# A two-layer decoder trunk on one core: convolution accumulators in alternating banks, a later first mean, a fixed order for the layer norm, one modulation part moved to TensorE, other distances between tiles

## The chip, the cores and the metric

The kernel is one program on one core of a Trainium2 chip. Its time is the device time of one execution in microseconds (us). Engine names are those of the profile: PE is TensorE, DVE is VectorE, ACT is ScalarE, POOL is GpSimd, SP is SyncE, which here only issues DMAs.

## The reference

The input x has 256 rows (T) of 2048 channels (D); c is one conditioning vector. Two layers follow each other, the first with a convolution module, the second with attention; each is followed by a gated feed-forward (ffn) of inner width 5632.

```python
shift, scale, gate = split(silu(c) @ mod_w + mod_b, 3)       # once for each of four sub-layers
h = rms_norm(x) * g * (1 + scale) + shift
# layer 0, convolution module
u = h @ pw1_w + pw1_b;  u = val * sigmoid(gt)                 # halves of u, 2048 channels each
u = causal_depthwise_conv(u, width 31) + b
u = silu(layer_norm(u) * ln_g + ln_b)
y = u @ pw2_w + pw2_b;  x = x + gate * y
# ffn of both layers
u = causal_depthwise_conv(h @ up_w, width 3) + b
x = x + gate * ((silu(gt) * val) @ down_w)
```

Layer 1's mixer is stick-breaking attention with 16 heads (products qk, v and o). A last rms_norm gives the output.

## The kernel before

**Layout.** Channels lie on the 128 partitions, the 256 rows along the free dimension. So an activation is KD = 16 tiles of 128x256 (the inner ffn 44), and a weight matrix is a stream of blocks of 128x128. Eight blocks make a piece of 512 KB; pieces are loaded in a fixed order (`load_next`, six buffers `raw`).

**Products.** All products but pw1 run in three passes of a reduced format: `split_next` makes wh on ACT (L225) and wl = raw - wh on DVE (L226), four buffers each; activations are split likewise (hh and hl for the modulated input, zh and zl for pw2's, gh and gl for the down product's, oh and ol for o's). `gemm` issues wh·xh (L269), wh·xl (L270), wl·xh (L271) for each block. After every piece `tick` drives side work: it adds a rate (0.7 for pw2) to a credit, and each full credit calls `advance` on the list `fill`, which takes one step of the first `pace["fills"]` generators in it.

**Modulations.** The product silu(c) @ mod_w is made in two ways. Column-wise (`mod_part`), each 128 outputs are one 1024 KB load (in_mt) and one DVE multiply-and-reduce (L294). Row-wise (`mod_rows`), each chunk is one 1024 KB load (in_mr) and four matmul pairs on PE (L505); sixteen chunks make 2048 outputs, after which one step copies the sums (ACT, L510) and one turns them into columns (PE L514, DVE L518). `ROWS` says how many groups of 512 outputs of ffn0's shift are made row-wise: 2 of 4 before; the other eight column tiles go through `mod_part("ffn0", 0, 8)`. The generator `mods0` makes layer 0's gate (16 chunks, two closing steps), ffn0's scale (the same) and ffn0's shift. Loads of both kinds share three buffers, `mraw`. All loads are issued by SP in program order (`load`), so a load that waits for its buffer holds those behind it.

**The convolution** (L634 to L716). The first eight of pw1's sixteen output tiles are computed ahead, with four more pieces in front of the loop. Then a loop over c = 0..16 runs, each pass in 19 steps s. Of a tile's 31 taps, ACT makes the first (`conv_first`, L591, into PSUM), 19 follow on DVE (`conv_tap`, L595, accumulating in PSUM), and eleven products are made by ACT (`conv_prod`, L603) and summed by POOL (L679, L681). DVE's taps of tile c alternate with the second half of tile c-1's. PE has in a pass two pieces of pw1 (L572, at s = 0 and 9), a generator step at s = 2, in even passes one more at s = 11, and sums for the layer norm's mean (`y_sum`, L616) and squares (L632). `conv_sum` (L607, at s = 3) finishes tile c-2. `first_mean` (ACT L619, DVE L620) takes the mean of the first eight tiles at the start of pass 10; after it `y_centre` (L624) subtracts it from three tiles a pass. The gate of tile i >= 8 (`gate_act` on ACT, `gate_mul` on DVE) comes in pass min(2(i-8)+2, i-1) at s = 12 and 15, and needs pw1's pieces of that tile.

The accumulators of the taps are halves of two PSUM banks (`conv_banks`): before, tiles 0 and 1 share one bank, 2 and 3 the other, 4 and 5 the first again. Dependencies between engines are kept by bank: who writes one half waits for what was issued before on the other.

**Order.** The framework schedules instructions by priority and simulated readiness, except where `in_order(here)` chains all instructions of an engine issued since `here`: the convolution loop runs exactly as written. Each engine executes its own queue in order.

**After the loop**, eight generator steps, the layer norm's rstd (L378), and sixteen z tiles: t = y * rstd on POOL (L734), t - dm on DVE (L735), silu on ACT (L736), split in zh (ACT L344) and zl (DVE L345). Then pw2 runs, its first eight output tiles interleaved over z; `pw2_done` (L745, L746) updates x and starts the next ffn's input (L359, L411, L412).

**Distances of tiles.** `SKEW` pads the tiles of a kind by multiples of eight columns, (high part, low part): this sets how far apart in a partition the tiles lie that PE streams one after the other. `h_tile` pads every tile to T + 8 columns and the last high one by 24 more.

Of the kernel before, what the change touches and what calls it, by code (L numbers as in the profile page):

```python
# [16 lines left out]
P = 128  # L17
# [8 lines left out]

SKEW = {"h": (3, 0), "z": (1, 7), "g0": (4, 4), "g1": (2, 6), "o": (0, 3)}
HEAD = 16
UBUFS = 9
M0 = 8  # L30
MOD_AHEAD = 2
ROWS = 2

# [76 lines left out]
def hybrid_trunk(ctx: ExitStack, tc: tile.TileContext, cfg: Cfg, io: dict):  # L110
# [16 lines left out]
    def psum_acc():  # L127
        return acc.tile([P, 512], F32, name="ps")
# [39 lines left out]
    fill = []  # L168
    pace = {"rate": 0.0, "credit": 0.0, "side": 0.0, "steps": 0.0, "heads": 2, "fills": 1}

# [135 lines left out]

    def mod_part(m, part, first=0, all_of_it=True):
        ahead = []
# [7 lines left out]
        if part == 1:  # L316
            mod_scale(m, 0, KD)
        if all_of_it:
            have.add((m, part))
        yield  # L320
# [136 lines left out]
    with ExitStack() as cv:  # L457
# [62 lines left out]
        def mods0():  # L520
# [7 lines left out]
            yield  # L528
            yield from mod_rows(*rows_of[2])

        gb = cpool.tile([P, KD], F32, name="gb")
# [4 lines left out]
        hf = [h_tile("hh", kt)[:, :T].bitcast(F32) for kt in range(KD)]  # L536
        act_tables("sigmoid_and_others")
# [49 lines left out]
        def conv_first(j):  # L587
            if len(conv_banks) < 2 and j % 2 == 0:
                conv_banks.append(psum_b())
            conv_ps[j] = conv_banks[j // 2 % 2][:, j % 2 * T:(j % 2 + 1) * T]  # L590
            nc.scalar.activation(conv_ps[j], us[j % UBUFS][:, PADW:], AF.Identity, bias=pc("cdb", j, 1),  # L591
                                 scale=tap(j, PADW))
# [4 lines left out]

        prods = {}

        def conv_prod(j, i):  # L600
            pr = h_tile("hl", sum(prods.values()) % PRODUCTS)[:, :T].bitcast(F32)
            prods[j] = prods.get(j, 0) + 1
            nc.scalar.activation(pr, us[j % UBUFS][:, i:i + T], AF.Copy, scale=tap(j, i))  # L603
            return pr
# [7 lines left out]

        def y_sum(j):
            if j in (0, M0):
                st["b"] = psum_acc()
            nc.tensor.matmul(st["b"][:, :T], ones_d, ys[j], start=j in (0, M0), stop=j in (M0 - 1, KD - 1))  # L616

        def first_mean():
            nc.scalar.activation(m1, st["b"][:, :T], AF.Copy, scale=KD / M0)  # L619
            nc.vector.tensor_tensor(dm, st["b"][:, :T], m1, op=ALU.subtract)  # L620
            st["sq"] = psum_acc()
# [37 lines left out]
        conv_first(0)  # L659
        for _ in range(4):  # L660
            pw1_piece(next(pw1))
        for c in range(KD + 1):
            late = gates_at.get(c, [])
            if c == M0 + 2:
                first_mean()
# [6 lines left out]
            for s in range(nd):  # L672
# [21 lines left out]
                if s in (6, 10, 14) and c > M0 + 1 and centred < c - 1:  # L694
                    y_centre(centred)
                    squares.append(centred)
                    centred += 1
# [24 lines left out]
        nc.vector.tensor_tensor(dm, dm, st["b"][:, :T], op=ALU.add)  # L722
        var = t256()
# [7 lines left out]
        zs = []  # L731
        for j in range(KD):
            t = t256()
            nc.gpsimd.tensor_tensor(t, ys[j], rs, op=ALU.mult)  # L734
            nc.vector.tensor_tensor(t, t, dm, op=ALU.subtract)  # L735
            nc.scalar.activation(t, t, AF.Silu, bias=pc("ln_b", j, 1), scale=pc("ln_g", j, 1))  # L736
# [14 lines left out]
        drain(fill)  # L751
        have.add(("ffn0", 0))
        pace["fills"] = 1

# [312 lines left out]
```

## Time and profile before

| | us |
|---|---|
| median of three runs | 2392.74 (2390.23 to 2392.78) |
| the profiled execution's own time | 2390.86 |
| its span in the profile | 2389.1 |
| PE busy in it | 2310.8 (97%) |
| DVE busy in it | 1759.0 (74%) |
| granted clock of PE, mean | 0.99 |
| DMA, mean over the span | 253 GB/s |

In a row of the timeline, the first number is the start in us from the span's start, the second the length of the stretch; then engine, line, operation, written tile <- read tiles, shapes, and xN, the number of merged instructions; in square brackets the engine's idle time before and what ended it. A 32-bit matmul (L572, L505, L616, L632) is two instructions. In a row of windows, the stretch is followed by its length, the busy time and count of PE, PE's weight loads, DVE, ACT and POOL, the granted clock, the DMA engines' busy share and GB/s. Matmul ends are modelled, so counts of matmuls in a window say more than PE's busy time.

### The profile page before, as it was taken

The numbers are of one execution on the slowest core, as the hardware profiler recorded it, in microseconds if no ns is written. First come the engines' busy times: TensorE is split into PE (matmuls) and PEld (weight loads), VectorE is DVE, ScalarE is ACT, GpSimd is POOL, SyncE is SP. The second block draws the span as 40 slices with busy tenths as digits, with TensorE's granted clock in tenths as the row PEclk, the third lists the DMA queues.
The fourth block names the chain that finished last, engine by engine and source line by source line (L and its number), as shares of the span: only waits on it lengthen the run. The fifth ranks groups of instructions, "written<-read, shape, count | busy, mean of one in ns | idle before, by whom it ended". The sixth has DMA issues, their size and how long they took to land.

```text
span 2389.1 us, 44051 instructions
## 1 busy us (share of the span) xinstructions
PE 2310.8 (97%) x17812; PEld 2199.8 (92%) x17812; DVE 1759.0 (74%) x2386; ACT 1157.1 (48%) x1761; POOL 281.4 (12%) x361
## 2 busy tenths in 40 slices
PE   7999878999999999999999999999999999999997
PEld 5877646999999999999998999999999999999997
DVE  7687886798878778788887676788876555666554
ACT  2054553665553345555465545556555434555543
POOL 4056641200000000000121000121000000000011
PEclk9999989999999999999999999999999999999999
DMA  9987578577769878778866666676865556555553
GB/s 393 425 323 294 191 274 336 184 272 274 275 242 349 310 270 287 265 277 310 316 232 246 241 248 243 240 270 232 292 211 186 187 188 187 186 186 186 186 186 106
DMA packets 138302, 603.55 MB, mean 253 GB/s; under 512 B 15345, under 2 KB 15473, under 8 KB 113521
## 3 DMA queue, kind: packets, MB, share of 16 engines
q1 hardware_dynamic: 138098, 600.74, 70.4%
q8 instruction: 139, 2.28, 0.4%
q14 instruction: 65, 0.53, 0.1%
HBM read 598.58 MB, written 2.10 MB: 251 GB/s over the span
## 4 chain that ended last, share of the span: by engine, by line
PE 85%; DVE 8%; DMA 3%; issue 2%; ACT 1%; POOL 0%; DVEq 0%; SPq 0%; ACTq 0%; POOLq 0%
PE ps L271 25%; PE ps L269 24%; PE ps L270 24%; PE ps L572 5%; DMA mraw<-in_mt_mix 2%; DVE auxb L595 2%; DVE mraw L294 2%; DVE wl L226 1%; PE ps L901 1%; PE ps L902 1%; PE ps L903 1%; PE auxa L505 1%; DMA mraw<-in_mt_ffn 1%; PE auxb L572 0%; DVE hl L345 0%
## 5 line engine op out<-in xcount | busy, mean ns | idle before, releaser
L225 ACT CAST wh<-raw 128x1024 fp32r<-128x1024 f32 x688 | 720.8, 1049 | 869.9 <-PE ps L270 665.5
L226 DVE TENSOR_TENSOR wl<-raw,wh 128x1024 fp32r<-128x1024 f32 x688 | 842.3, 1227 | 396.1 <-ACT wh L225 385.8
L271 PE MATMUL ps<-hh,wl 128*128 128x256 f32 (+1 forms) x3328 | 937.8, 282 | 4.4 <-DVE wl L226 4.4
L270 PE MATMUL ps<-hl,wh 128*128 128x256 f32 (+1 forms) x3328 | 937.0, 282 | 3.0 <-DVE hl L345 1.5
L269 PE MATMUL ps<-hh,wh 128*128 128x256 f32 (+1 forms) x3328 | 936.0, 281 | 0.0
L271 PEld LDWEIGHTS ps<-hh,wl 128*128 128x128 f32 x3328 | 627.5, 189 | 5.0 <-DVE wl L226 5.0
L270 PEld LDWEIGHTS ps<-hl,wh 128*128 128x128 f32 x3328 | 627.8, 189 | 3.9 <-DVE hl L345 2.0
L269 PEld LDWEIGHTS ps<-hh,wh 128*128 128x128 f32 x3328 | 628.8, 189 | 0.4
L294 DVE CUSTOM_DVE_ANT_0 mraw<-mraw,csr 128x2048 f32<-128x2048 f32 x152 | 348.5, 2293 | 89.2 <-DMA mraw<-in_mt_mix 54.1
L271 PE MATMUL ps<-gh,wl 128*128 128x256 f32 x1408 | 399.7, 284 | 0.0
L269 PE MATMUL ps<-gh,wh 128*128 128x256 f32 x1408 | 397.7, 282 | 0.0
L270 PE MATMUL ps<-gl,wh 128*128 128x256 f32 x1408 | 393.5, 280 | 0.0
L270 PEld LDWEIGHTS ps<-gl,wh 128*128 128x128 f32 x1408 | 266.9, 190 | 0.0
L269 PEld LDWEIGHTS ps<-gh,wh 128*128 128x128 f32 x1408 | 266.0, 189 | 0.0
L271 PEld LDWEIGHTS ps<-gh,wl 128*128 128x128 f32 x1408 | 264.6, 188 | 0.0
L363 POOL TENSOR_TENSOR sumsq<-sumsq,t 128x256 f32<-128x256 f32 x56 | 59.8, 1068 | 1593.5 <-ACT t L359 1593.3
L572 PE MATMUL ps<-hh,raw 128*128 128x256 f32 x832 | 191.3, 383 | 0.0
L572 PEld LDWEIGHTS ps<-hh,raw 128*128 128x128 f32 x832 | 159.3, 192 | 27.8 <-issue 3.4
L770 DVE SCALAR_TENSOR_TENSOR t<-ps,par,t 128x254 f32<-128x254 f32 x336 | 160.2, 478 | 4.1
L595 DVE SCALAR_TENSOR_TENSOR auxb<-u,cpar,auxb 128x256 f32<-128x256 f32 x304 | 138.4, 485 | 8.9 <-ACT auxb L591 3.8
L681 POOL TENSOR_TENSOR y<-y,hl 128x256 f32<-128x256 f32 x144 | 108.4, 753 | 22.0 <-ACT hl L603 11.2
L767 ACT ACTIVATE t<-ps,par 128x256 f32<-128x256 f32 x168 | 93.7, 559 | 0.0
(168 smaller groups left out, 2120.9 us busy)
## 6 DMA issues: line engine op xcount, KB each, us to landing
raw<-in_w_down SPq DMA_DIRECT2D x176, 512.0 KB, 3.9
mraw<-in_mt_mix SPq DMA_DIRECT2D x80, 1024.0 KB, 8.0
mraw<-in_mt_ffn SPq DMA_DIRECT2D x72, 1024.0 KB, 6.0
raw<-in_w_pw SPq DMA_DIRECT2D x96, 512.0 KB, 7.0
raw<-in_w_up01b SPq DMA_DIRECT2D x84, 512.0 KB, 5.0
raw<-in_w_up11b SPq DMA_DIRECT2D x84, 512.0 KB, 3.5
raw<-in_w_up00b SPq DMA_DIRECT2D x80, 512.0 KB, 4.5
raw<-in_w_up10b SPq DMA_DIRECT2D x80, 512.0 KB, 3.6
```

What stands on the lines that cost most here:

```text
L225: nc.scalar.copy(wh[:, :n], v[:, :n])
L226: nc.vector.tensor_tensor(wl[:, :n], v[:, :n], wh[:, :n].bitcast(F32), op=ALU.subtract)
L269: nc.tensor.matmul(o, wh[:, c], xh[kt], start=first, stop=False, skip_group_check=halves > 0)
L270: nc.tensor.matmul(o, wh[:, c], xl[kt], start=False, stop=False, skip_group_check=halves > 0)
L271: nc.tensor.matmul(o, wl[:, c], xh[kt], start=False, stop=left[nb] == 0, skip_group_check=halves > 0)
L294: nc.vector.tensor_tensor_reduce(out=v, in0=v, in1=csr, scale=1.0, scalar=0.0, op0=ALU.mult, op1=ALU.add, accum_out=macc[:, nb:nb + 1])
L363: engine.tensor_tensor(self.sum, self.sum, sq, op=ALU.add)
L572: nc.tensor.matmul(banks[j][:, nb // KD * T:(nb // KD + 1) * T], w[:, b * P:(b + 1) * P], hf[kt], start=first, stop=left[j] == 0, skip_gro ...
L595: nc.vector.scalar_tensor_tensor(conv_ps[j], us[j % UBUFS][:, k:k + T], tap(j, k), conv_ps[j], op0=ALU.mult, op1=ALU.add)
L681: nc.gpsimd.tensor_tensor(ys[c], ys[c], pr, op=ALU.add)
L767: nc.scalar.activation(y, ps[:, :T], AF.Identity, bias=pc(f"fdb{i}", nb, 1), scale=w(FW - 1))
L770: nc.vector.scalar_tensor_tensor(y[:, s:], ps[:, :T - s], w(k), y[:, s:], op0=ALU.mult, op1=ALU.add)
```

## The change

- The accumulators of tiles j and j+1 lie in different banks: tile j takes bank j % 2, half (j // 2) % 2.
- The first mean comes one pass later (pass 11), with a sum tile of its own for each half; centring starts a pass later too.
- Two pieces of pw1 instead of four stand ahead of the loop; passes 0 to 14 take two each.
- Every pass takes two generator steps instead of two and one by turns.
- ffn0's shift is made row-wise as a whole (`ROWS = 4`: 16 chunks instead of 8, no `mod_part`), one generator step at a time.
- After the loop six generator steps, behind dm * rstd, then the z loop, now inside `in_order`, with the first two multiplications on DVE and the split of tile j-2 issued behind the silu of tile j.
- Other `SKEW` values; the h tiles have T + 2 columns and are made in turns (hh0, hl0, hh1, ...).

```diff
-SKEW = {"h": (3, 0), "z": (1, 7), "g0": (4, 4), "g1": (2, 6), "o": (0, 3)}
+SKEW = {"z": (1, 1), "g0": (1, 1), "g1": (7, 3), "o": (3, 7)}
-ROWS = 2
+ROWS = 4
...
-            advance(fill, pace["fills"])
+            advance(fill, 1)
...
-    def h_tile(n, i):
-        pad = SKEW["h"][n == "hl"] if i == KD - 1 else 0
-        return hpool.tile([P, T + 8 + pad * 8], F32R, name=f"{n}{i}")[:, :T + 2]
-
     def h_tiles(i):
-        return [h_tile(n, i) for n in ("hh", "hl")]
+        return [hpool.tile([P, T + 2], F32R, name=f"{n}{i}") for n in ("hh", "hl")]
...
-            if len(conv_banks) < 2 and j % 2 == 0:
+            if len(conv_banks) < 2:
                 conv_banks.append(psum_b())
-            conv_ps[j] = conv_banks[j // 2 % 2][:, j % 2 * T:(j % 2 + 1) * T]
+            conv_ps[j] = conv_banks[j % 2][:, j // 2 % 2 * T:(j // 2 % 2 + 1) * T]
...
         def first_mean():
-            nc.scalar.activation(m1, st["b"][:, :T], AF.Copy, scale=KD / M0)
-            nc.vector.tensor_tensor(dm, st["b"][:, :T], m1, op=ALU.subtract)
+            nc.scalar.activation(m1, st[0][:, :T], AF.Copy, scale=KD / M0)
+            nc.vector.tensor_tensor(dm, st[0][:, :T], m1, op=ALU.subtract)
...
-        for _ in range(4):
+        for _ in range(2):
             pw1_piece(next(pw1))
...
-            if c == M0 + 2:
+            if c == M0 + 3:
                 first_mean()
...
-                if c < KD - 2 and s in (0, nd // 2):
+                if c < KD - 1 and s in (0, nd // 2):
                     pw1_piece(next(pw1))
-                if c < KD and (s == 2 or s == nd // 2 + 2 and c % 2 == 0):
+                if c < KD and s in (2, nd // 2 + 2):
                     advance(fill, 1)
...
-        in_order(here)
-        for _ in range(8):
-            advance(fill, 1)
-        fill.append(mod_part("ffn0", 0, 4 * cfg.rows0, all_of_it=False))
-        pace["fills"] = 2
...
+        for _ in range(6):
+            advance(fill, 1)
...
-        for j in range(KD):
-            t = t256()
-            nc.gpsimd.tensor_tensor(t, ys[j], rs, op=ALU.mult)
-            nc.vector.tensor_tensor(t, t, dm, op=ALU.subtract)
-            nc.scalar.activation(t, t, AF.Silu, bias=pc("ln_b", j, 1), scale=pc("ln_g", j, 1))
-            zs.append([skewed(zpool, "z", n == "zl", f"{n}{j}") for n in ("zh", "zl")])
-            split_act(t, *zs[j])
+        for j in range(KD + 2):
+            if j < KD:
+                zt.append(t256())
+                (nc.vector if j < 2 else nc.gpsimd).tensor_tensor(zt[j], ys[j], rs, op=ALU.mult)
+                nc.vector.tensor_tensor(zt[j], zt[j], dm, op=ALU.subtract)
+                nc.scalar.activation(zt[j], zt[j], AF.Silu, bias=pc("ln_b", j, 1), scale=pc("ln_g", j, 1))
+            if j > 1:
+                zs.append([skewed(zpool, "z", n == "zl", f"{n}{j - 2}") for n in ("zh", "zl")])
+                split_act(zt[j - 2], *zs[j - 2])
+        in_order(here)
```

More of the change, by code (lines that the diff above doesn't have):

```diff
@@ L168, in hybrid_trunk @@
     fill = []
-    pace = {"rate": 0.0, "credit": 0.0, "side": 0.0, "steps": 0.0, "heads": 2, "fills": 1}
+    pace = {"rate": 0.0, "credit": 0.0, "side": 0.0, "steps": 0.0, "heads": 2}
     def advance(gens, k):
@@ L305, in mod_scale, with mod_part @@
                                        pc(gname[m], k0, n), op0=ALU.add, op1=ALU.mult)
-    def mod_part(m, part, first=0, all_of_it=True):
+    def mod_part(m, part, first=0):
         ahead = []
@@ L317, in mod_part @@
             mod_scale(m, 0, KD)
-        if all_of_it:
-            have.add((m, part))
+        have.add((m, part))
         yield
@@ L529, in mods0 @@
             yield from mod_rows(*rows_of[2])
+            have.add(("ffn0", 0))
         gb = cpool.tile([P, KD], F32, name="gb")
@@ L535, in hybrid_trunk @@
             nc.gpsimd.tensor_tensor(ys[kt], xs[kt], rs, op=ALU.mult)
-        hf = [h_tile("hh", kt)[:, :T].bitcast(F32) for kt in range(KD)]
+        htiles = [h_tiles(kt) for kt in range(KD)]
+        hf = [v[0][:, :T].bitcast(F32) for v in htiles]
+        spare = [v[1] for v in htiles]
         act_tables("sigmoid_and_others")
@@ L596, in conv_tap @@
                                            op0=ALU.mult, op1=ALU.add)
-        prods = {}
+        prods = []
         def conv_prod(j, i):
-            pr = h_tile("hl", sum(prods.values()) % PRODUCTS)[:, :T].bitcast(F32)
-            prods[j] = prods.get(j, 0) + 1
+            v = spare.pop(0) if spare else hpool.tile([P, T + 2], F32R, name=f"hl{len(prods) % PRODUCTS}")
+            prods.append(v)
+            pr = v[:, :T].bitcast(F32)
             nc.scalar.activation(pr, us[j % UBUFS][:, i:i + T], AF.Copy, scale=tap(j, i))
@@ L613, in y_sum @@
         def y_sum(j):
+            b = j >= M0
             if j in (0, M0):
-                st["b"] = psum_acc()
-            nc.tensor.matmul(st["b"][:, :T], ones_d, ys[j], start=j in (0, M0), stop=j in (M0 - 1, KD - 1))
+                st[b] = psum_acc()
+            nc.tensor.matmul(st[b][:, :T], ones_d, ys[j], start=j in (0, M0), stop=j in (M0 - 1, KD - 1))
         def first_mean():
-            nc.scalar.activation(m1, st["b"][:, :T], AF.Copy, scale=KD / M0)
-            nc.vector.tensor_tensor(dm, st["b"][:, :T], m1, op=ALU.subtract)
+            nc.scalar.activation(m1, st[0][:, :T], AF.Copy, scale=KD / M0)
+            nc.vector.tensor_tensor(dm, st[0][:, :T], m1, op=ALU.subtract)
             st["sq"] = psum_acc()
@@ L693, in hybrid_trunk @@
                     y_sum(c - 2)
-                if s in (6, 10, 14) and c > M0 + 1 and centred < c - 1:
+                if s in (6, 10, 14) and c > M0 + 2 and centred < c - 1:
                     y_centre(centred)
@@ L715, in hybrid_trunk @@
         act_tables("sqrt_and_others")
[L716 to L722 removed]
+        nc.vector.tensor_tensor(dm, dm, st[1][:, :T], op=ALU.add)
         var = t256()
@@ L751, in hybrid_trunk @@
         drain(fill)
-        have.add(("ffn0", 0))
-        pace["fills"] = 1
     def ffn(i, entry, out):
```

2 lines of the change are left out of this document (1 added, 1 removed).

## The prediction

> **What bounds the kernel now.** I read the page first, then windows of equal matmul work, then the chain of waits and the timeline of the first 460 us, where all edits but the distances of tiles lie.
>
> ```profile
> span 2389.1 us, 44051 instructions
> PE 2310.8 (97%) x17812; PEld 2199.8 (92%) x17812; DVE 1759.0 (74%) x2386; ACT 1157.1 (48%) x1761; POOL 281.4 (12%) x361
> ```
>
> TensorE (PE) carries the kernel: 78 us of its span are idle. So an edit pays in two ways: it shortens a stretch where PE waits (the end of the convolution, the second pointwise product pw2), or it shortens the matmuls themselves. What is gained before the first ffn moves all that follows.
>
> The convolution, VectorE (DVE) alone, passes c = 2 and 3 (conv_sum, L607, stands at step 3 of each pass); then ACT's conv_first in it:
>
> ```profile
> 155.53 0.42 DVE L607 TENSOR_TENSOR y<-y,auxb 128x256 f32<-128x256 f32 x1
> 155.87 3.22 DVE L595 SCALAR_TENSOR_TENSOR auxb<-u,cpar,auxb 128x256 f32<-128x256 f32 x8
> 159.34 1.66 DVE L595 SCALAR_TENSOR_TENSOR auxb<-u,cpar,auxb 128x256 f32<-128x256 f32 x4 [0.24 <-ACT auxb L591]
> 160.91 0.48 DVE L581 SCALAR_TENSOR_TENSOR u<-ps,cpar,t 128x256 f32<-128x256 f32 x1
> ...
> 164.57 0.41 DVE L607 TENSOR_TENSOR y<-y,auxb 128x256 f32<-128x256 f32 x1
> 164.91 9.40 DVE L595 SCALAR_TENSOR_TENSOR auxb<-u,cpar,auxb 128x256 f32<-128x256 f32 x19
> 174.41 0.42 DVE L607 TENSOR_TENSOR y<-y,auxb 128x256 f32<-128x256 f32 x1
> ...
> 158.74 0.57 ACT L591 ACTIVATE auxb<-u,cpar 128x256 f32<-128x256 f32 x1 [5.66 <-DVE auxb L595]
> ```
>
> In even passes the two tiles whose taps alternate lie in different banks: 8 taps in 3.22 us, 0.4025 each. In odd passes they share one: 19 taps in 9.40, 0.495. conv_first of a tile waits for the tap before it in its bank, and the next tap there waits 0.24 for it; so far that is in even passes only. A pair of passes takes DVE 18.88 (155.53 to 174.41).
>
> PE in the same stretch:
>
> ```profile
> 136.24 20.72 PE ps L572 x96
> ...
> 174.28 1.06 PE L505 MATMUL auxa<-mraw,hot 128*32 128x512 f32 x8
> 175.28 0.70 PE L616 MATMUL ps<-y,ones_d 128*128 128x256 f32 x2
> 175.81 3.62 PE L572 MATMUL ps<-hh,raw 128*128 128x256 f32 x16
> ...
> 180.35 3.72 PE L572 MATMUL ps<-hh,raw 128*128 128x256 f32 x16
> ...
> 185.54 7.07 PE L572 MATMUL ps<-hh,raw 128*128 128x256 f32 x32
> 192.54 1.05 PE L505 MATMUL auxa<-mraw,hot 128*32 128x512 f32 x6
> ```
>
> PE never stops: a pair of passes takes 18.26 (174.28 to 192.54): four pieces of pw1 (16 matmuls each, 3.45 back to back), three chunks of the row-wise modulation (L505), two sums. It runs behind DVE, since four pieces (13.8) go ahead of its pass 0. Where DVE needs PE it therefore stands still:
>
> ```profile
> 240.92 0.42 DVE L620 TENSOR_TENSOR dm<-ps,m 128x256 f32<-128x256 f32 x1 [11.55 <-ACT m L619]
> ...
> 248.44 0.58 ACT L510 COPY rows<-auxa 128x512 f32<-128x512 f32 x1 [3.97 <-PE auxa L505]
> 255.75 0.95 PE L514 MATMUL auxa<-cst,rows 128*128 128x4 f32 x8
> 256.73 0.18 DVE L518 TENSOR_TENSOR v_mix<-auxa,cpar 128x16 f32<-128x16 f32 x1 [2.06 <-PE auxa L514]
> ...
> 319.95 0.42 DVE L607 TENSOR_TENSOR y<-y,auxb 128x256 f32<-128x256 f32 x1
> 327.34 5.08 POOL L734 TENSOR_TENSOR t<-y,rstd 128x256 f32<-128x256 f32 x6 [14.50 <-DVE rstd L378]
> 331.16 1.20 PE L269 MATMUL ps<-zh,wh 128*128 128x256 f32 x4 [5.87 <-POOL t L734]
> ```
>
> 11.55 us at the first mean (start of pass 10), 2.06 at the end of the first modulation rows (pass 11). From 257 on PE waits for DVE, whose last conv_sum ends at 320.4; the layer norm's rstd is there at 327.2 (call it T), pw2 begins at 331.2.
>
> **The change part by part.** Sums run against the profiled execution: 2390.9 us, 1.8 more than its span; the three runs' median is 2392.7.
>
> *Convolution.* (a) With neighbours in two banks every pass gets the even passes' rate: 19 x 0.4025 = 7.65, conv_sum 0.34 (start to start), the 0.25 for conv_first now in every pass: 8.24, and 8.64 with a gate (0.40): 16.9 a pair, not 18.88. (b) Two pieces instead of four ahead of the loop: pass 0 of PE starts 6.9 earlier, at 146.3; passes 0 to 14 keep two pieces each. (c) A second modulation chunk in odd passes: a chunk between two pieces costs 1.0 (174.28 to 175.28) and the two restarts 0.2 (2 x 3.65 for the split pair, 7.1 unsplit), so PE's pair becomes 19.4, 9.7 a pass. PE, not DVE, now sets the pace: pass 2 at 164.7 (two passes of 9.2), pass 8 at 223.0.
>
> (d) The new pace of the generator moves its sync points: its 17th and 18th steps (ACT's copy L510; L514, L518) come in pass 8, where they stood in passes 10 and 11. This is a wait put in place of the one removed. DVE would be at step 11 of pass 8 at 208 (step 3 of pass 2 at 153.7, 1.8 earlier than in the row above as pass 1 is quicker too, + 6 x 8.45 + 3.6 for eight taps and conv_sum); but ACT's copy waits for PE's 16th chunk (222.9), with the products and gates of pass 8 queued behind it, and L518 waits on DVE for L514, after PE's second piece of pass 8: 232.0. All of DVE's taps queue behind L518, and it loses 24 us; PE has its sums already and loses nothing. The first mean, a pass later, then waits for nothing.
>
> From there both engines go in step, with these pieces of work besides:
>
> ```profile
> L226 DVE TENSOR_TENSOR wl<-raw,wh 128x1024 fp32r<-128x1024 f32 x688 | 842.3, 1227 | 396.1 <-ACT wh L225 385.8
> ...
> L632 PE MATMUL ps<-t,ones_d 128*128 128x256 f32 x32 | 9.7, 429 | 0.5 <-ACT t L628 0.5
> ```
>
> DVE, with 3 centrings (as conv_sum, 0.34 each) a pass from pass 11 and weight splits (L226, 1.23) in passes 13 and 14, starts pass 9 at 235.7 (seven taps and a gate after L518), then 243.9, 252.6, 262.3, 271.9, and pass 14 at 282.8. PE: 232.0, 243.0, 253.1, 263.2, then with three squares' sums (two instructions each, about 0.5) a pass 274.8 and 286.4; the last piece, in pass 14, ends at 295.3, and tile 15's gate waits 3 us for it. DVE starts pass 15 at 298, 16 at 307.5, and ends its last conv_sum at 312.8: **-7.6**. Another 0.5 comes as the chunks at 319 no longer stand before PE's last sum. If taps stay at 0.495 in half the passes nothing is gained here; if the gate's wait vanishes and PE keeps 9.1 a pass, some 12.
>
> *Layer norm and pw2.*
>
> ```profile
> L735 DVE TENSOR_TENSOR t<-t,dm 128x256 f32<-128x256 f32 x16 | 11.2, 747 | 3.8 <-POOL t L734 3.8
> L736 ACT ACTIVATE t<-t,cpar 128x256 f32<-128x256 f32 x16 | 9.0, 596 | 7.1 <-DVE t L735 7.0
> L344 ACT CAST zh<-t 128x256 fp32r<-128x256 f32 x16 | 5.6, 396 | 0.0
> L345 DVE TENSOR_TENSOR zl<-t,zh 128x256 fp32r<-128x256 f32 x16 | 5.9, 411 | 0.0
> ...
> L269 PE MATMUL ps<-zh,wh x256: 276/280/579, 331.2 to 456.5; 128*128 128x256 f32 x128
> ...
> PE ps L271 <- DVE wl L226: 6.0, 5, 2.1
> PE ps L269 <- ACT wh L225: 4.6, 2, 3.0
> PE ps L269 <- ACT t L745: 3.0, 4, 1.4
> ...
> 371.00:381.00 10.00, 9.84 (x82) 8.65 (x80) 6.10 (x5) 2.23 (x3) 0.00 (x0) 1.00 1.02 426
> ```
>
> Six generator steps stand before the z loop now: L510 waits for ACT's table load, L514 for it, L518 holds DVE: +1.7. In the fixed order split j-2 comes behind tile j on both engines, so subtraction, silu, copy, difference follow one another: 0.42 to 0.75 + 0.60 + 0.40 + 0.41, about 2.0 a tile, where the free order made 16 tiles in 20 us. The first z comes at T + 5.3; PE uses one per 2.8 us (24 matmuls), so it is still served, if the weight splits get into the gaps (rival 1).
>
> Behind it, before, each generator step of pw2 drove two generators at 0.7 a piece: 0.5 + 1.4 MB per piece of 2.83 + 0.7 x 1.1 = 3.6 us, 528 GB/s where the DMA is full at 426. The eight shift tiles also held DVE 2.3 us each (L294). After: one chunk a step, 1.2 MB in 3.6 us, 333 GB/s, and no L294. These 1024 KB loads go past SP's same queue as the weights, in step with PE. PE's own sum: 768 matmuls at 0.1177, 90.4; 14 chunks at 1.1, 15.4; L514 1.0. Before, 90.4, ten chunks (11.0), two L514 (1.9) and the 13.6 us of waits above left 8.5 of the 125.4 for restarts and lower clock; I keep 3 of those and 4 of the waits. So 113.8 from T + 5.3, or T + 119.1; before it was T + 129.4: **-10.3**. No wait at all would give -14, the weights held back +1.5.
>
> *Distances of tiles.* Windows inside single products, only the moving operand's tiles differing (gh of layer 0, hh, gh of layer 1, oh, zh):
>
> ```profile
> 740.00:800.00 60.00, 60.00 (x502) 60.00 (x502) 46.62 (x47) 22.03 (x21) 0.00 (x0) 1.00 0.92 343
> 900.00:1000.00 100.00, 100.00 (x849) 100.00 (x848) 81.11 (x104) 50.93 (x72) 0.00 (x0) 1.00 0.79 277
> 1940.00:2000.00 60.00, 60.00 (x512) 60.00 (x511) 29.53 (x30) 22.05 (x21) 0.00 (x0) 1.00 0.60 187
> 1540.00:1580.00 40.00, 40.00 (x341) 40.00 (x340) 35.02 (x55) 22.53 (x48) 9.16 (x8) 1.00 0.69 243
> 425.00:455.00 30.00, 30.00 (x255) 30.00 (x255) 19.55 (x31) 17.61 (x35) 3.80 (x6) 1.00 0.66 212
> ```
>
> 119.5, 117.8, 117.2, 117.3, 117.6 ns a matmul, all at full granted clock and PE never idle. No row shows the new distances, so each stage lies between 117.2 and 119.5. I take the common value, 117.8, for all: layer 0's down products (2112) gain 3.6, layer 1's (2112) lose 1.2, o (768) loses 0.4, up and q, k (9984) stay: **-2.0**. All at 117.2 would give -11, all at 119.5 +25.
>
> The Trainium skill speaks against any such effect: "SBUF — State Buffer", section "Who interferes with whom", has it that only the port pair of VectorE and GpSimd contends and that PE never waits for anyone. By that rule this term is 0 and the sum 2 higher; the 2 per cent between stages stay unexplained by it.
>
> Sum: -7.6 - 0.5 - 10.3 - 2.0 = -20.4 on 2390.9: **2370.5, say 2371**.
>
> **Rivals.**
> 1. *The z loop holds the weights back.* Two us a tile end it at T + 36, and if pw2's splits from the fourth piece on stay behind it on ACT and DVE, PE stands from T + 19 to T + 36 (it stood 3 us there). pw2's gain becomes +1.5: **2382**. For it: before, ACT did four splits in a row only after the last z. Against: the new order leaves gaps of about 1 us in each tile.
> 2. *Distances do nothing* (the stages differ by something else, such as the DMA's load, 0.92 against 0.60 in the rows above): **2373**. The page named above would have it so. Against: o at 0.69 and layer 1 at 0.60 run alike.
> 3. *All stages reach 117.2 or less*: -11 instead of -2: **2362**.
> 4. *Not the bank.* Odd passes keep 0.495 for another reason: 1.75 more in every other pass, the convolution ends where it did: **2378**.
> 5. *Slower*: hh and hl, laid in turns now, and the others fall to layer 0's 119.5: 1.75 x 9984 + 2.3 x 2112 + 2.0 x 1536 ns = +25 in place of -2: **2398**. It decides from 119.4 ns on hh. Against: hh runs at 117.8 in each product that reads it.
>
> **How the numbers follow.** The forecast (2365 to 2377) 0.42; rivals 0.16, 0.14, 0.12, 0.08, 0.08 in order. 0.2% (4.8 us) is about what a measurement of this kernel can tell from no change. A quarter of rival 1 and half of rival 4, met by a small loss of matmul rate, end within it: same 0.08; rival 5 slower 0.08; faster 0.84. The range runs from rival 3 with no waits left in pw2 to rival 1 with layer 0's rate on part of the matmuls: 2354 to 2389; rival 5 and the ends of 3 stay out.
>
> **What would show it.** Right: L595 near 0.40 in all passes; no wait at L620, but some 20 us on DVE at L518 in pass 8; the last conv_sum near 313; z tiles 2 us apart; pw2 without L294, the DMA under 400 GB/s, its end near T + 119; about 509 matmuls in 60 us in layer 0's down products. Wrong: 19 taps still in 9.4; PE idle 10 us or more in the z loop; hh at fewer than 845 matmuls in 100 us.

## The result, and the profile after

The changed kernel takes 2357.39 us (median of 4 runs, 2351.95 to 2359.09) against 2392.76 for the kernel before (4 runs, 2390.23 to 2392.90): a ratio of 0.9851, 95% interval 0.9833 to 0.9868. That is 35.4 us less, where 20.4 were forecast; 2357 lies in the range (2354 to 2389) and beyond the likeliest case's own (2365 to 2377). Most of the 15 us by which the forecast fell short lies in one term, the distances of tiles.

The profiled execution took 2359.09 us, its span is 2356.9, 32.2 less than before. The head of the page:

```profile
span 2356.9 us, 44169 instructions
PE 2300.1 (98%) x17876; PEld 2182.0 (93%) x17876; DVE 1723.7 (73%) x2371; ACT 1160.4 (49%) x1761; POOL 282.4 (12%) x359
```

PE makes 64 more instructions (eight chunks of the shift) and is yet busy 10.7 us less: its matmuls became shorter. DVE lost 15 instructions and 35 us (the slow taps, L294).

**Convolution.** VectorE in passes 2 to 3 and in pass 8 of the changed kernel (its lines: taps L593, conv_sum L606, conv_first L589, gate L579, generator L513), then the first mean, the gate of tile 15 and the last conv_sum; below them PE's last piece of pw1:

```profile
154.42 0.41 DVE L606 TENSOR_TENSOR y<-y,auxb 128x256 f32<-128x256 f32 x1
154.87 3.62 DVE L593 SCALAR_TENSOR_TENSOR auxb<-u,cpar,auxb 128x256 f32<-128x256 f32 x9
158.74 1.27 DVE L593 SCALAR_TENSOR_TENSOR auxb<-u,cpar,auxb 128x256 f32<-128x256 f32 x3 [0.25 <-ACT auxb L589]
...
163.05 0.41 DVE L606 TENSOR_TENSOR y<-y,auxb 128x256 f32<-128x256 f32 x1
163.50 3.62 DVE L593 SCALAR_TENSOR_TENSOR auxb<-u,cpar,auxb 128x256 f32<-128x256 f32 x9
...
232.73 0.18 DVE L513 TENSOR_TENSOR v_mix<-auxa,cpar 128x16 f32<-128x16 f32 x1 [22.93 <-PE auxa L509]
...
253.40 0.42 DVE L620 TENSOR_TENSOR dm<-ps,m 128x256 f32<-128x256 f32 x1
...
296.52 0.47 DVE L579 SCALAR_TENSOR_TENSOR u<-ps,cpar,t 128x256 f32<-128x256 f32 x1
...
313.13 0.42 DVE L606 TENSOR_TENSOR y<-y,auxb 128x256 f32<-128x256 f32 x1
```

```profile
290.31 3.62 PE L570 MATMUL ps<-hh,raw 128*128 128x256 f32 x16
```

Nine taps in 3.62 us, 0.402 each, in even and odd passes alike, with 0.25 for conv_first in each. The 24 us at the generator's step in pass 8 are there (22.93), and the first mean waits for nothing; nor does the gate, since PE's last piece had ended at 293.9. The last conv_sum ends at 313.55; 312.8 was forecast, 320.37 it was before.

**Layer norm and pw2.** VectorE after the last sum, then pw2's first product of each block (L269) from its first to its last start, with that of the ffns behind it:

```profile
318.50 1.75 DVE L373 RECIPROCAL rstd<-t 128x256 f32<-128x256 f32 x1 [0.57 <-ACT t L371]
...
327.82 0.42 DVE L340 TENSOR_TENSOR zl<-t,zh 128x256 fp32r<-128x256 f32 x1 [0.96 <-ACT zh L339]
328.16 0.42 DVE L732 TENSOR_TENSOR t<-t,dm 128x256 f32<-128x256 f32 x1
329.54 0.43 DVE L340 TENSOR_TENSOR zl<-t,zh 128x256 fp32r<-128x256 f32 x1 [0.96 <-ACT zh L339]
...
333.89 0.42 DVE L340 TENSOR_TENSOR zl<-t,zh 128x256 fp32r<-128x256 f32 x1
...
336.08 1.23 DVE L226 TENSOR_TENSOR wl<-raw,wh 128x1024 fp32r<-128x1024 f32 x1 [1.43 <-ACT wh L225]
337.22 0.42 DVE L340 TENSOR_TENSOR zl<-t,zh 128x256 fp32r<-128x256 f32 x1
```

```profile
L269 PE MATMUL ps<-hh,wh x3328: 274/280/467, 438.9 to 2217.1; 128*128 128x256 f32 x184, 128*128 128x258 f32 x12
...
L269 PE MATMUL ps<-zh,wh x256: 274/280/551, 326.2 to 438.6; 128*128 128x256 f32 x128
```

rstd is there at 320.25 (T). A z tile takes 1.72 us (327.82 to 329.54); with a weight split in its gap it takes longer, here 3.33 (333.89 to 337.22, L226 at 336.08 between). Over all sixteen the mean is 2.06, where about 2.0 was forecast. pw2 begins at T + 5.95 and ffn0 at 438.9, T + 118.65 (forecast T + 119.1); before, ffn0 began at 456.8. So 17.9 us of the 32.2 are won ahead of ffn0 (18.4 forecast), the other 14.3 behind it, where only the distances differ.

**Matmuls.** Windows of the changed kernel inside the products whose windows stand in the prediction, in the same order (gh of layer 0, hh, gh of layer 1, oh), then zh:

```profile
720.00:780.00 60.00, 60.00 (x513) 60.00 (x512) 47.14 (x47) 22.26 (x22) 0.00 (x0) 1.00 0.92 337
870.00:970.00 100.00, 100.00 (x860) 100.00 (x859) 84.50 (x109) 51.76 (x71) 0.00 (x0) 1.00 0.78 280
1900.00:1960.00 60.00, 60.00 (x510) 60.00 (x509) 29.25 (x29) 22.40 (x22) 0.00 (x0) 1.00 0.58 185
1510.00:1550.00 40.00, 40.00 (x341) 40.00 (x340) 33.41 (x53) 21.69 (x46) 8.59 (x7) 1.00 0.70 248
...
395.00:425.00 30.00, 30.00 (x252) 27.09 (x251) 20.30 (x39) 19.05 (x45) 5.95 (x6) 1.00 0.57 179
```

Layer 0's gh went from 502 to 513 matmuls in 60 us, hh from 849 to 860 in 100, layer 1's gh from 512 to 510; oh is the same. A window also counts the two or three matmuls that lie across its ends, so a spacing read from it is too small, by 0.4 ns for the 100 us of hh and by 0.9 for the 40 us of oh. From the starts of neighbouring matmuls in the trace:

| spacing, ns | before | after |
|---|---|---|
| hh, up products | 118.16 | 116.68 |
| gh, layer 0 | 120.0 | 117.5 |
| gh, layer 1 | 117.8 | 118.1 |
| zh | 118.3 | 117.7 |
| oh | 118.25 | 118.25 |

### The profile page after: what moved, and what is told of

The parts are those of the page before. It is cut to its first block, busy times and chain, and to the rows that moved or that the text cites. A ratio compares the mean times of both kernels' runs of the same rounds, so it can differ in the third digit from the quotient of the medians.

```text
span 2356.9 us, 44169 instructions
## 1 busy us (share of the span) xinstructions
PE 2300.1 (98%) x17876; PEld 2182.0 (93%) x17876; DVE 1723.7 (73%) x2371; ACT 1160.4 (49%) x1761; POOL 282.4 (12%) x359
## 4 chain that ended last, share of the span: by engine, by line
PE 85%; DVE 8%; DMA 3%; ACT 2%; issue 2%; POOL 0%; SPq 0%; DVEq 0%; ACTq 0%; POOLq 0%
PE ps L269 25%; PE ps L270 25%; PE ps L271 25%; PE ps L570 3%; DMA mraw<-in_mt_mix 3%; DVE auxb L593 2%; DVE mraw L294 2%; PE auxa L500 1%; PE ps L898 1%; PE ps L899 1%; PE ps L900 1%; DVE wl L226 1%; ACT wh L225 0%; DVE hl L340 0%; PE auxa L830 0%
## 5 line engine op out<-in xcount | busy, mean ns | idle before, releaser
L226 DVE TENSOR_TENSOR wl<-raw,wh 128x1024 fp32r<-128x1024 f32 x688 | 842.9, 1228 | 399.0 <-ACT wh L225 390.9
L269 PE MATMUL ps<-hh,wh 128*128 128x256 f32 (+1 forms) x3328 | 935.2, 281 | 0.0
L269 PEld LDWEIGHTS ps<-hh,wh 128*128 128x128 f32 x3328 | 626.7, 188 | 0.3
L269 PE MATMUL ps<-gh,wh 128*128 128x256 f32 x1408 | 394.0, 280 | 0.0
L294 DVE CUSTOM_DVE_ANT_0 mraw<-mraw,csr 128x2048 f32<-128x2048 f32 x144 | 329.8, 2290 | 83.6 <-DMA mraw<-in_mt_mix 50.5
L269 PEld LDWEIGHTS ps<-gh,wh 128*128 128x128 f32 x1408 | 265.9, 189 | 0.0
L593 DVE SCALAR_TENSOR_TENSOR auxb<-u,cpar,auxb 128x256 f32<-128x256 f32 x304 | 126.0, 482 | 4.2 <-ACT auxb L589 3.3
```

The source lines that it names most:

```text
L226: nc.vector.tensor_tensor(wl[:, :n], v[:, :n], wh[:, :n].bitcast(F32), op=ALU.subtract)
L269: nc.tensor.matmul(o, wh[:, c], xh[kt], start=first, stop=False, skip_group_check=halves > 0)
L294: nc.vector.tensor_tensor_reduce(out=v, in0=v, in1=csr, scale=1.0, scalar=0.0, op0=ALU.mult, op1=ALU.add, accum_out=macc[:, nb:nb + 1])
L593: nc.vector.scalar_tensor_tensor(conv_ps[j], us[j % UBUFS][:, k:k + T], tap(j, k), conv_ps[j], op0=ALU.mult, op1=ALU.add)
```

## The experiments

Theory: the bank mapping gave the convolution's 7 us, the rearranged chunks and z tiles pw2's 10, and the distances 14 by making each matmul shorter. The rivals are that distances do nothing, that the taps' rate is not the bank's, and that pw2's gain came from one of its edits alone. Each run changes the changed kernel unless said otherwise.

| run | undone | ffn0 starts | median of n runs (lowest to highest) | ratio to before, 95% |
|---|---|---|---|---|
| changed kernel | nothing | 438.9 | 2357.39 of 4 (2351.95 to 2359.09) | 0.9833 to 0.9868 |
| old_distances | distances | 438.9 | 2371.72 of 4 (2368.96 to 2374.98) | 0.9893 to 0.9926 |
| before_distances | all but the distances | 459.8 | 2376.06 of 4 (2374.27 to 2376.83) | 0.9911 to 0.9940 |
| old_banks | banks | 447.7 | 2364.27 of 4 (2360.21 to 2367.75) | 0.9864 to 0.9894 |
| mean_early | later first mean | 436.8 | 2355.76 of 4 (2351.85 to 2359.98) | 0.9832 to 0.9858 |
| two_generators | shift on TensorE | 436.3 | 2356.38 of 4 (2354.78 to 2356.94) | 0.9831 to 0.9860 |
| free_z | fixed z order | 440.7 | 2361.61 of 4 (2359.04 to 2362.92) | 0.9851 to 0.9880 |
| old_pace | two generator steps a pass | 446.8 | 2362.03 of 4 (2360.75 to 2367.51) | 0.9862 to 0.9888 |
| old_pw2 | the last three together | 452.0 | 2366.88 of 4 (2365.41 to 2371.09) | 0.9870 to 0.9903 |
| aligned | (new distances) | 436.9 | 2333.02 of 6 (2326.91 to 2358.49) | 0.9734 to 0.9807 |

### The distances undone (old_distances), and alone on the kernel before (before_distances)

```diff
-SKEW = {"z": (1, 1), "g0": (1, 1), "g1": (7, 3), "o": (3, 7)}
+SKEW = {"h": (3, 0), "z": (1, 7), "g0": (4, 4), "g1": (2, 6), "o": (0, 3)}
...
-        htiles = [h_tiles(kt) for kt in range(KD)]
-        hf = [v[0][:, :T].bitcast(F32) for v in htiles]
-        spare = [v[1] for v in htiles]
+        hf = [h_tile("hh", kt)[:, :T].bitcast(F32) for kt in range(KD)]
+        spare = [h_tile("hl", kt) for kt in range(KD)]
```

> The changed kernel with the distances of the tiles (h, z, g, o) as before; all else as changed. Theory A, the distances made the matmuls shorter: every product goes back to the spacing it had before (hh 118.2 ns in place of 116.7, layer 0's gh 120.0 in place of 117.5, zh 118.3 in place of 117.7, oh 118.25 and layer 1's gh 117.8 in place of 118.1), which over 9984, 2112, 768, 768 and 2112 matmuls is 14 us: about 2371. Theory B, the distances do nothing and the stages run faster for another reason, such as the other order of the loads: spacing as in the changed kernel and 2357.

2371.72, 14.3 more than the changed kernel. ffn0 starts where it did (438.9), so all of it lies behind. hh is back at 849 matmuls in 100 us:

```profile
880.00:980.00 100.00, 100.00 (x849) 100.00 (x848) 82.31 (x107) 50.34 (x70) 0.00 (x0) 1.00 0.76 277
```

The reverse edit, on the kernel before:

> The kernel before with the changed kernel's distances of tiles alone. Theory A, the distances act by themselves through the matmuls' spacing, whatever else the kernel does: 14 us less than the kernel before, 2378.5. Theory B, the gain needs the changed kernel's other edits: 2393.

2376.06 against 2393.42 for the kernel before beside it: 17 us less, by the interval 14 to 21. The same window now holds 859:

```profile
880.00:980.00 100.00, 100.00 (x859) 100.00 (x859) 86.27 (x111) 52.41 (x72) 0.00 (x0) 1.00 0.78 289
```

Theory A in both. In the faster row the DMA, DVE and ACT do a little more than in the slower one, so less work beside the matmuls is not the cause.

### The distances by themselves (distances_alone, equal_alone)

```python
for i in range(ROUNDS * KD):                      # one case: d, p, a
    h0 = U * (a + 7 + (64 + p) * (i % KD))        # U = 8 columns = 32 bytes
    l0 = h0 + U * (32 + d)
    ...
    nc.tensor.matmul(o, wh, hx[:, h0:h0 + T], ...)
    nc.tensor.matmul(o, wh, hx[:, l0:l0 + T], ...)
    nc.tensor.matmul(o, wl, hx[:, h0:h0 + T], ...)
```

> Leaves out the whole computation: only products wh*xh, wh*xl, wl*xh from tiles that stand in SBUF from the start, 15360 matmuls in 160 cases of 96. The cases differ only in where the tiles lie: the distance from xh to xl and the pitch from tile to tile, both modulo 256 bytes in steps of 32, and the start. Nothing else works beside them. Theory A (distances): the spacing is fixed for each case and differs between cases by 3 to 6 ns, as 116.7 and 120.0 in the products; the pattern repeats with the tile number in a period set by the pitch. Theory B: all cases within 0.3 ns of each other, about 117.

The cases run from 113.3 to 120 ns, and one stands at 121.2; 137 of the 160 lie between 117 and 119. Three windows inside cases with all distances a multiple of 256 bytes, the tiles starting 0, 160 and 192 bytes (modulo 256) behind the start of the weights:

```profile
27.00:37.00 10.00, 10.00 (x86) 10.00 (x85) 0.00 (x0) 0.37 (x1) 0.00 (x0) 1.00 0.00 0
85.00:95.00 10.00, 10.00 (x88) 10.00 (x87) 0.00 (x0) 0.00 (x0) 0.00 (x0) 1.00 0.01 2
95.20:105.20 10.00, 10.00 (x91) 10.00 (x90) 0.00 (x0) 0.33 (x1) 0.00 (x0) 1.00 0.01 2
```

86, 88 and 91 matmuls in the same 10 us, by their starts 120.0, 117.3 and 113.33 ns, while DVE and POOL do nothing, ACT next to nothing, at most 2 GB/s are transferred and the granted clock is 1.00. Theory A, in that the cases differ by up to 7.9 ns where nothing but addresses does; each case ran once, so this run does not show that a case's spacing is fixed.

In the changed kernel the pattern can be seen matmul by matmul. Its h tiles lie 1056 bytes apart, so hh to hh is 2112, which is 64 modulo 256: a period of four tiles. Starts from one matmul to the next in up01b, the mean of its last 25 repeats (standard deviation 0.4 ns at most):

| tile modulo 4 | wh·xh to wh·xl | to wl·xh | to the next block |
|---|---|---|---|
| 0 | 120.0 | 116.8 | 116.0 |
| 1 | 117.2 | 115.0 | 115.8 |
| 2 | 118.0 | 121.0 | 112.0 |
| 3 | 116.0 | 116.0 | 116.2 |

Tiles 4 to 15 repeat these four rows; before, where hh to hh was 1056 bytes (32 modulo 256), the period was eight tiles.

equal_alone keeps all distances a multiple of 256 and varies where the weights start, too:

> Leaves out the whole computation, as the run of distances alone: products wh*xh, wh*xl, wl*xh from tiles in SBUF, here with all moving tiles at equal distance modulo 256 bytes (their start at one of 8 places, 32 bytes apart), the weights at one of 8, and each such case begun four times behind a matmul of another width (50, 84, 120, 250 columns); 256 cases of 48 matmuls. Theory A, the addresses alone set the spacing: the four begins of a case agree, 113.3 ns for start 224 with weights at 32, another value for each other pair. Theory B, one pair of addresses has two lasting spacings, 113.3 and 117.8, and what came before decides: the four begins of a case disagree in many cases.

| start of the moving tile minus start of the weights, bytes modulo 256 | spacing behind the four begins, ns |
|---|---|
| 0 | 120.0 |
| 32 | 116.7 or 117.8 |
| 64 | 117.8 (once 113.3) |
| 96 | 120.0 |
| 128 | 118.6 to 118.8, in three begins 120.0 |
| 160 | 117.2 to 118.8, once 120.0 |
| 192 | 113.3 in 21 of 32 begins, 117.8 in 11 |
| 224 | 118.2 to 118.5 |

Each row holds for all eight places of the weights, so of the two addresses only the difference counts. The run's first two begins are left out: their matmuls are mixed in time, and part of them start 213 ns apart. At 0, 96 and 224 the begins agree, at the others they don't all: there one pair of addresses has two lasting spacings, as theory B has it, and at 192, the fastest, above all. That what came before decides, its other half, is not shown: at 192 both values occur behind each of the four widths.

### The distances made equal (aligned)

```diff
-SKEW = {"z": (1, 1), "g0": (1, 1), "g1": (7, 3), "o": (3, 7)}
+LEAD = {'h': 6, 'hend': 2, 'g0': 2, 'g1': 2, 'z': 4, 'o': 2}
+HPAD = 64
...
-        return [hpool.tile([P, T + 2], F32R, name=f"{n}{i}") for n in ("hh", "hl")]
+        return [hpool.tile([P, T + HPAD], F32R, name=f"{n}{i}")[:, :T + 2] for n in ("hh", "hl")]
...
-        return pool.tile([P, T + 8 * SKEW[kind][low]], F32R, name=name)[:, :T]
+        return pool.tile([P, T], F32R, name=name)
```

LEAD puts so many times 32 bytes ahead of the first tile of a kind.

> The changed kernel with other distances again: all h, z, g and o tiles start at 224 modulo 256 bytes (the weights at 32, as they are), so each distance is a multiple of 256 bytes; that case ran at 113.33 ns a matmul in the run of distances alone, the best of its 160. Theory A, the distances alone set the spacing: 8448 up products of hh 3.35 ns shorter, 4224 of gh 4.5, 1536 of zh and oh 4.7: 28 + 19 + 7 = 54 us, 2303 (the q, k and v stage, which did not follow its matmuls, left out). Theory B, transfers and the other engines disturb it in a whole kernel, and 116 ns is the least: 2344. Theory C, it does nothing: 2357.

2333.02, the fastest kernel here (24 us less than the changed one), but neither 2303 nor 2344 in kind, and its runs lie 32 us apart. Two windows of hh products in its one profiled execution (2348.13 us), one in layer 0 and one in layer 1:

```profile
500.00:560.00 60.00, 60.00 (x532) 60.00 (x531) 52.22 (x69) 32.78 (x46) 0.00 (x0) 1.00 0.80 294
...
1980.00:2040.00 60.00, 60.00 (x512) 60.00 (x511) 38.87 (x54) 30.71 (x43) 0.00 (x0) 1.00 0.54 186
```

The same tiles at the same addresses: 532 matmuls, then 512; by their starts 113.33 and 117.78, the two values that equal_alone shows for this difference. It keeps 113.33 for most of the first 1000 us and changes to 117.78 at about 997. In the q, k and v stage, where other matmuls break hh's stream into stretches, it goes back and forth, and a stretch keeps its value to the end: of the twelve stretches of more than 40 matmuls from 1270 us on, eight run at 113.3 and four at 117.8. Seven us inside one of each, 62 matmuls and 64, with the DMA alike:

```profile
1292.00:1299.00 7.00, 7.00 (x62) 7.00 (x61) 5.59 (x8) 4.21 (x7) 0.54 (x2) 1.00 0.89 344
1368.00:1375.00 7.00, 7.00 (x64) 7.00 (x63) 5.43 (x7) 3.96 (x7) 0.54 (x2) 1.00 0.91 348
```

From about 1500 us to the end it is 117.78, although less is transferred and computed beside it than in layer 0. What tips it is open.

### The banks undone (old_banks)

```diff
-            if len(conv_banks) < 2:
+            if len(conv_banks) < 2 and j % 2 == 0:
...
-            conv_ps[j] = conv_banks[j % 2][:, j // 2 % 2 * T:(j // 2 % 2 + 1) * T]
+            conv_ps[j] = conv_banks[j // 2 % 2][:, j % 2 * T:(j % 2 + 1) * T]
```

> The changed kernel, only conv_first's banks as before: tiles 2k and 2k+1 in one bank. Theory A, the bank decides: odd passes take 0.495 us a tap again, even ones 0.40. Up to pass 8 DVE has over 20 us in hand at the modulation's step, so only passes 9 to 16 count, four of them odd by 1.75 us each: the last conv_sum 7 us later, at 320, and 2364. Theory B, the taps were slow in odd passes for another reason (such as conv_first's place in the pass): 0.40 in all passes and 2357. Theory C: taps slow again, but the end of the convolution is set by TensorE, so 2357 to 2359.

2364.27, 6.9 more. An odd pass, the beginning of the even one behind it, and the last conv_sum:

```profile
239.54 8.88 DVE L593 SCALAR_TENSOR_TENSOR auxb<-u,cpar,auxb 128x256 f32<-128x256 f32 x18
248.53 0.42 DVE L606 TENSOR_TENSOR y<-y,auxb 128x256 f32<-128x256 f32 x1
248.86 3.23 DVE L593 SCALAR_TENSOR_TENSOR auxb<-u,cpar,auxb 128x256 f32<-128x256 f32 x8
...
321.60 0.42 DVE L606 TENSOR_TENSOR y<-y,auxb 128x256 f32<-128x256 f32 x1
```

18 taps in 8.88 (0.493), then 8 in 3.23 (0.404). The end of the convolution is 8.5 later (321.60 against 313.13), a little more than the four odd passes' 7.0. Theory A: without this edit more than the whole gain of the convolution (6.8) is gone.

### The first mean a pass earlier (mean_early)

```diff
-            if c == M0 + 3:
+            if c == M0 + 2:
...
-                if s in (6, 10, 14) and c > M0 + 2 and centred < c - 1:
+                if s in (6, 10, 14) and c > M0 + 1 and centred < c - 1:
```

> The changed kernel with the first mean a pass earlier, at the start of pass 10, as before. Theory A, by then VectorE and TensorE are in step, as the modulation's step of pass 8 has already held VectorE: no wait over 1 us at the first mean, and 2357. Theory B, the 11.55 us wait comes back, since TensorE's sum of the tile stands two pieces behind: the last conv_sum up to 9 us later, 2366.

2355.76, within the spread. VectorE at the two places:

```profile
233.01 0.18 DVE L513 TENSOR_TENSOR v_mix<-auxa,cpar 128x16 f32<-128x16 f32 x1 [22.93 <-PE auxa L509]
...
245.01 0.41 DVE L620 TENSOR_TENSOR dm<-ps,m 128x256 f32<-128x256 f32 x1
```

No wait at L620. The later first mean brings nothing, since the generator's step has taken that wait over, in pass 8 and twice as long as the 11.55 us of before.

### pw2's edits undone (two_generators, free_z, old_pace, old_pw2)

```diff
-ROWS = 4
+ROWS = 2
...
-            advance(fill, 1)
+            advance(fill, pace["fills"])
...
+        fill.append(mod_part("ffn0", 0, 4 * cfg.rows0))
+        pace["fills"] = 2
```

> The changed kernel, but half of ffn0's shift back on VectorE: two rows in place of four on TensorE, and in pw2 two generator steps at a time. Theory A, pw2 was held by its loads (528 GB/s wanted) and by L294's products: pw2 takes 125 us in place of 112.7, the end 10 later: 2368. Theory B, pw2 got shorter by the other order of the layer norm, and the chunks on TensorE cost what the loads cost: pw2 loses the time of 8 chunks (8.8 us) and nothing comes in place: 2349. Between them, 2357, if both are equal.

2356.38: no difference. PE's waits from the last sums to the end of pw2, in us, times, longest, and a window of 10 us in pw2:

```profile
PE ps L271 <- DVE wl L226: 4.9, 5, 2.2
PE ps L269 <- ACT t L745: 2.2, 3, 0.8
PE ps L269 <- ACT zh L339: 1.0, 1, 1.0
```

```profile
371.00:381.00 10.00, 7.14 (x54) 6.33 (x53) 9.30 (x12) 6.64 (x13) 3.25 (x2) 1.00 1.02 413
```

The loads do hold PE: 413 GB/s with a DMA share of 1.02, PE busy 7.1 of 10 us. In the changed kernel the same window has 357 GB/s, and of these waits only the one for zh is left, ahead of pw2's first matmul:

```profile
371.00:381.00 10.00, 10.00 (x73) 6.95 (x72) 4.17 (x6) 5.21 (x9) 0.73 (x1) 1.00 0.96 357
```

```profile
PE ps L269 <- ACT zh L339: 1.3, 1, 1.3
```

But without the edit PE is spared eight chunks in pw2. From row to row of the groups, x48 here and x112 in the changed kernel, eight matmuls a chunk:

```profile
L500 PE MATMUL auxa<-mraw,hot 128*32 128x512 f32 x48 | 6.4, 604 | 0.0
```

```profile
L500 PE MATMUL auxa<-mraw,hot 128*32 128x512 f32 x112 | 16.0, 605 | 0.0
```

9.6 us of matmuls more against some 7 us of waits less: ffn0 starts 2.6 later with the edit than without. Between the theories, nearest to "equal".

```diff
         act_tables("silu_and_others")
...
+        in_order(here)
         early.close()
...
                 split_act(zt[j - 2], *zs[j - 2])
-        in_order(here)
```

> The changed kernel, only the layer norm's part behind the last sum (the z tiles and their splits) in free order again, as the scheduler puts it. Theory A, the fixed order lets the weight splits into the gaps between the z tiles and so took pw2's waits away: in free order the four weight splits come only after the last z, TensorE waits some 6 to 10 us in pw2, 2364 to 2367. Theory B, the order of the z tiles does nothing, since TensorE uses a z tile in 2.8 us and each order makes one in less: 2357.

2361.61, 4.2 more; the intervals overlap, so the time alone does not settle it. ffn0 starts 1.8 later; PE's waits in pw2 are 2.0 for wh, 0.8 for zh and 0.4 for wl. Of theory A's 6 to 10 us little is seen: the order was worth about 2.

```diff
-                if c < KD and s in (2, nd // 2 + 2):
+                if c < KD and (s == 2 or s == nd // 2 + 2 and c % 2 == 0):
```

> The changed kernel, but the convolution advances the generator three times in two passes, as before, not twice a pass: about 8 chunks fewer on TensorE before the layer norm, 8 more in pw2, and the modulation's step that held VectorE in pass 8 comes in passes 10 and 11. Theory A, chunks beside the convolution are hidden and chunks in pw2 cost their 1.1 us each: about 9 more, 2366. Theory B, the wait at that step costs the convolution what the chunks gain: 2357 or a few us less.

2362.03, 4.6 more, with intervals that overlap a little. VectorE at the generator's step and at the last conv_sum, then the starts of the products:

```profile
251.14 0.18 DVE L513 TENSOR_TENSOR v_mix<-auxa,cpar 128x16 f32<-128x16 f32 x1 [2.86 <-PE auxa L509]
...
309.48 0.42 DVE L606 TENSOR_TENSOR y<-y,auxb 128x256 f32<-128x256 f32 x1
```

```profile
L269 PE MATMUL ps<-hh,wh x3328: 274/280/467, 446.8 to 2219.4; 128*128 128x256 f32 x184, 128*128 128x258 f32 x12
...
L269 PE MATMUL ps<-zh,wh x256: 274/280/582, 322.1 to 442.8; 128*128 128x256 f32 x128
```

Both theories hold a part. The step holds VectorE 2.86 us in place of 22.93, and the convolution ends 3.65 earlier; pw2 pays 12 more for the chunks that are left (322.1 to 446.8, with 4 us of chunks behind its last product). ffn0 starts 7.9 later; some 4 come back in the up products ahead of the first down product (261.9 us long, not 265.9). In the changed kernel PE waits 3.1 us there for a weight split, and behind the wait matmuls start 213 ns apart at a lower granted clock; 30 matmuls of the stage come late by about 3.0 us in all, in old_pace three by 0.3, and the longest gap there is 1.5. The changed kernel's window behind its wait:

```profile
478.00:484.00 6.00, 6.00 (x34) 6.00 (x34) 3.73 (x8) 2.77 (x6) 0.00 (x0) 0.60 0.55 176
```

The three together:

> The changed kernel with three of its edits undone together: three generator steps in two passes, the free order of the z tiles, and half of the shift on VectorE with two generators in pw2. Alone they made 2362.0, 2361.6 and 2356.4 against 2357.4. Theory A, they add up: 4.6 + 4.2 - 1.0 = 7.8 more, 2365. Theory B, each of them alone covers for the others, and together pw2's waits (13.6 us before the change) come back: ffn0 starts 10 to 11 us later, 2368.

2366.88; ffn0 starts 13.1 later than in the changed kernel, where the three alone add up to 7.1 (7.9 + 1.8 - 2.6).

```profile
PE ps L269 <- ACT wh L225: 5.4, 4, 3.3
PE ps L271 <- DVE wl L226: 4.0, 3, 1.9
PE auxa L501 <- DMA mraw<-in_mr_ffn: 3.0, 1, 3.0
```

Theory B: weights and chunks come late again, 12.4 us in three rows. The medians alone (9.5 more, where adding up gives 7.8) could not tell the theories apart; ffn0's start, in one execution of each kernel, does. A likely reason, for which no pair was undone: with two steps a pass in the convolution pw2 is left 6 chunks when the shift alone is undone, and 14 when all three are, so the other edits could be undone alone for little.

## Why the prediction was right or wrong

- **Convolution, -7.6 forecast, -6.8 measured: right**, and for its reason. old_banks puts the taps back to 0.493 and the end 8.5 later. VectorE's 24 us at the generator's step came as 22.93. One step was off: the forecast had both engines in step behind it, with 3 us of waiting at tile 15's gate. That gate did not wait for TensorE, whose last piece ended at 293.9, while VectorE reached the gate only at 296.52; from pass 9 to the last conv_sum VectorE waited 2.2 us in all, so its own work set the end, 0.75 later than forecast. That fewer pieces of pw1 stand ahead of the loop was not undone by itself.
- **First mean: right** that it waits for nothing; mean_early adds that it would not have waited a pass earlier either.
- **Layer norm and pw2, -10.3 forecast, -10.9 measured from T (129.6 before, 118.7 after): the size was right, in part by luck, since the cause was right only in part.** PE's waits in pw2, 13.6 us before, did go, and pw2 did get 14 chunks (before it had nine, not ten). The step put this down to loads of 528 GB/s and to L294. two_generators shows the loads' price (some 7 us of waits), but undoing the shift brings as much back by eight chunks fewer on TensorE. What carries the gain is the pace in the convolution, which takes chunks out of pw2 (old_pace: ffn0 7.9 later), together with the other two (old_pw2: 13.1). Rival 1 did not happen: the weight splits went into the gaps of the z tiles, and TensorE stood 1.3 us there. Of the 0.5 for the chunks ahead of PE's last sum 0.1 came: rstd stood 6.8 us behind the last conv_sum before, and stands 6.7 behind it now.
- **Distances, -2.0 forecast, -14.3 measured: the mis-sized term.** That the distances act was right, and rival 2, which makes the term 0, is out: old_distances and before_distances move the time by 14 and 17 us, and distances_alone shows 113.3 to 120 ns at full clock with no other engine at work. The rule of the Trainium skill, "SBUF — State Buffer", section "Who interferes with whom", that PE never waits for anyone, is about other engines; these runs speak against the reading that a term of 0 follows from it. (The section also calls PE's read ports for the moving operand and for the weights independent of each other; equal_alone fits that badly, since there the spacing follows the difference of the two addresses. Whether the ports are the cause was not tested.) What failed is the step "No row shows the new distances, so each stage lies between 117.2 and 119.5. I take the common value, 117.8, for all": rows with other distances set no bound. hh, with most of the matmuls, went to 116.68, below every row of before on the same scale (117.8 the least): 8448 matmuls of the up products, which became 9.6 us shorter in all (238.2 to 235.2 in layer 0's second). gh of layer 0 gave 5.2 (two stages of 126.7 to 124.2 and 124.0), gh of layer 1 lost 0.7. The q, k and v stage stayed (260.1 to 260.2 behind its first product), although its hh matmuls went from 118.45 to 117.27 there; why was not tried. Rival 3 came nearest, and even it was too small, though not all stages became as fast as it says. The windows also misled in one point: they made oh and layer 1's gh look alike, which stands against rival 2 in the prediction, but by their starts these ran at 118.25 and 117.8.
- **Sum.** On the spans, -17.9 ahead of ffn0 (-18.4 forecast) and -14.3 behind it (-2.0), -32.2 in place of -20.4.

## What to carry to other kernels

Where one engine streams back to back, look at the starts of single instructions, tile by tile: a pattern that repeats with the tile number says that addresses set the rate, and a loop over addresses alone measures it in one run, which no row of the old kernel can. Where work is moved from a stage, follow it to where it lands: here chunks moved into the convolution paid, because the matmul engine was not the last one there, and the edit that looked like pw2's cure (the shift) put chunks back and was by itself worth nothing. A wait of 23 us on an engine that has that much in hand costs little (with 2.86 us of it, in old_pace, the convolution ended only 3.65 earlier), and it can make another edit, the later mean, worthless.

## What the runs showed of the hardware that was not expected

- The spacing of three-pass 128x128x256 matmuls from SBUF depends on the start of the moving tile minus that of the weights, modulo 256 bytes: 113.3 to 120.0 ns with equal distances (equal_alone).
- One and the same set of addresses can have two lasting spacings, 113.33 and 117.78 (192 bytes, equal_alone). In a whole kernel it changed from the one to the other and back (aligned, whose runs take 2327 to 2358 us); what decides is open.
- Taps on VectorE that alternate between accumulators in one PSUM bank take 0.493 us, in two banks 0.40, without any wait in the trace.
